# A hybrid decoder step: two head pairs of the prompt scan in one burst, the sample-diagonal products in a run of their own, and broadcasts from zero-padded rows

## The chip, the cores and the metric

The kernel runs on one NeuronCore of a Trainium2 chip. The metric is the device time of one execution in microseconds (us), lower is better.

## What is computed

Two layers of a hybrid trunk for 256 prompt tokens and 8 x 4 sample tokens, which share all weights. Each layer is a half-step SwiGLU feed-forward, a mixer of three branches (causal pooling, a Mamba-2 scan, attention into 256 memory tokens), and a second half-step feed-forward. The change touches the scan (`ssd_scan`), in chunks of 128 tokens, 16 heads of 64 channels, 4 groups of B and C with state 128:

```
xdt   = x * dt
decay = exp(where(causal, acum_t - acum_s, -inf))
y_diag = einsum('bcghts,bcsghp->bctghp', (C B^T) * decay, xdt)   # inside a chunk
states = einsum('bcsgn,bcsghp->bcghpn', B, xdt * to_end)         # the chunk's state
y = y_diag + y_off + D * x
```

The prompt has two chunks and no earlier state. The sample group has four new tokens for each of eight sequences, and an earlier state that is read for `y_off`.

## The kernel before

All activations lie as [128 channels, 288 tokens] (256 prompt, then 32 sample tokens). The 128x128 weight tiles are streamed past TensorE in slabs of eight. Each weight and each activation is split into two float32r parts, so one weight tile takes three products of 288 columns; the trace names them `ps`. Every slab is a tick (`Stream.tick`): ScalarE and VectorE split a later slab (`whi`, `wlo`), and `Stream.step` then advances each piece of side work that is under way by one stage (one `yield`), in the order in which the pieces were started. A piece may be started with a delay in ticks. The order on each engine is the order in which the program issues it (`manual_schedule`).

The scan's side work starts with the pooling columns (`kind == "u"`, `c == 0`), L1154 to L1158: `xss_work` after 3 ticks, the eight `sample_state` pieces from 8 on, `heads4(g)` after 4, 8, 12 and 16 ticks, `sample_y` after 28 and `group_norm` after 30. The ticks of the pooling columns (`pool_mix`) and of the `z` and gate columns run at the same time. `heads4(g)` takes the four heads of one group in two pairs, stage by stage:

1. four transposes of x (`ps_x`) and `rows(0)`
2. `xd = x * dt` and `xw` on VectorE and GpSimd, `clamp(0)`, `rows(1)`
3. `clamp(1)` on VectorE, the exponentials of both pairs on ScalarE (`E`)
4. the mask and C B^T multiplied into both `E` on VectorE
5. `outputs(0)` on TensorE
6. `finish(0)`, `outputs(1)`
7. `finish(1)`

Stage 5 of one group falls into the tick of stage 1 of the next. `rows(pi)` broadcasts two rows of `nst` (48 partitions: the high part of the cumulative sums in rows 0 to 15, the low part in 32 to 47) to all partitions, by two float32r products with a selecting column of `sel2` as weights. `outputs(pi)` writes one PSUM bank `ps_y`: two sample-diagonal products (`Ms`, 32 rows x 64 columns of the array, 32 tokens moving), six products with `E` (128 x 64, 128 tokens moving) that alternate between the halves j = 0 and 1 of the output partitions, and two products of full size for the state (`Bt`). A product of float32 operands shows as two passes in the trace, one of float32r as one. `finish(pi)` adds `D * x` on VectorE, copies the state out on ScalarE and issues its DMA on the queue of SP, which also issues the weight loads.

PSUM has seven banks under tag `b` for all of this and one under tag `a`. `dt_work` fills `nst`; GpSimd clears it there first, in each layer.

Of the kernel before, what the change touches and what calls it, by code (L numbers as in the profile page):

```python
# [44 lines left out]
def group_order(tiles, cuts):  # L45
    """Weight tiles (tile, k) of a group of products: all tiles up to each cut of k in turn."""
    for a, b in zip((0,) + cuts[:-1], cuts):
        for t in tiles:
            for k in range(a, b):
                yield t, k  # L50
# [56 lines left out]
class Stream:  # L107
    """Runs the packed weight tiles past TensorE, each split into two float32r parts.

    Every SLAB tiles make a tick: the split of a later slab is issued, then one stage  # L110
    of every piece of side work that is under way."""

# [8 lines left out]
    def parts(self, n):  # L121
        """The first slab comes in two halves, so that the products can begin."""
        k = 2 if n == 0 else 1
        return [slice(j * SLAB * P // k, (j + 1) * SLAB * P // k) for j in range(k)]
# [64 lines left out]
def trunk_kernel(ctx, tc, wpack, xT, memT, vecs, consts, wdt, wpool, hpool, hconv, h0T, kT, vC,  # L189
# [31 lines left out]
    def blocks(name):  # L221
        """Two tiles of zeros for block_fill()."""
        us = [unit(f"{name}{j}") for j in range(2)]
        for u in us:
            G.memset(u, 0.0)
        return us

    def block_fill(us, srcs, copy):
        """Block b of 32 columns, of each of the four slices, gets the slice's samples with all but sample b zero."""
        for u, src in zip(us, srcs):  # L230
            copy(u.rearrange("p a (b s) -> p a b s", b=DB)[:, :, :, 0:DL], src.rearrange("p a (b t) -> p a b t", b=DB))
# [55 lines left out]
    def chunk(units, c):  # L287
        return units[c // 2][:, c % 2, :]

    def products(tiles, cuts, xs):  # L290
        """One PSUM bank per tile: W[:, cols].T @ x."""
        ps = [bank("ps") for _ in tiles]
        for j, k in group_order(range(len(tiles)), cuts):
            mm3(ps[j][:, :T], W.take(), chunk(xs[0], k), chunk(xs[1], k), k == 0, k == cuts[-1] - 1)
        return ps
# [9 lines left out]
    def rstd_cols(accs, starts, width, name):  # L305
        """1 / sqrt(mean + eps) of the column sums of accs, tokens on partitions: [128, len(accs) * len(starts)]."""
        n = len(accs) * len(starts)
        ps = bank("ps_" + name)
        for a, acc in enumerate(accs):
            for j, s in enumerate(starts):  # L310
                k = a * len(starts) + j
                mm(ps[:, k:k + 1], acc[:, s:s + P], ones[:, 0:1])
        v = sp.tile([P, 12], F32, tag="rs_v", name="rs_v", bufs=2)[:, :n]
        ts(v, ps[:, :n], 1.0 / width, ALU.mult, EPS, ALU.add)
        r = sp.tile([P, 12], F32, tag="rs_r", name="rs_r", bufs=2)[:, :n]
        act(r, v, AF.Sqrt)
        V.reciprocal(out=r, in_=r)
        stt(v, v, -0.5, r, ALU.mult, ALU.mult)
        tt(v, v, r, ALU.mult)
        stt(r, v, 1.5, r, ALU.add, ALU.mult)  # L320
        return r

    def rstd_rows(r, t, sums, width):
        """r = 1 / sqrt(sums / width + eps), elementwise; stages."""
        yield
        ts(t, sums, 1.0 / width, ALU.mult, EPS, ALU.add)
        act(r, t, AF.Sqrt)
        yield
        V.reciprocal(out=r, in_=r)
        stt(t, t, -0.5, r, ALU.mult, ALU.mult)  # L330
        tt(t, t, r, ALU.mult)
        stt(r, t, 1.5, r, ALU.add, ALU.mult)
# [3 lines left out]
    def spread(r):  # L336
        """out[p, t] = r of token t, for every partition p; r holds tokens 0.., 128.., 160.. by column."""
        ps = bank("ps_spread")
        mm(ps[:, 0:P], r[:, 0:1].to_broadcast([P, P]), ident)
        mm(ps[:, P:TP], r[:, 1:2].to_broadcast([P, P]), ident)  # L340
        mm(ps[:, TP:T], r[:, 2:3].to_broadcast([P, P]), ident[:, P - TS:P])
        return ps

    class Norm:
        """Collects sum(x^2) chunk by chunk and splits x * gain for the products."""

# [22 lines left out]
    class Final:  # L369
        """The last norm: x * gain in place, then its scale and the output."""  # L370

# [38 lines left out]

# [1 line left out]
    mem = [unit(f"mem{j}") for j in range(KC // 2)]  # L412
# [16 lines left out]
    rv = cp.tile([P, 2], F32, name="rv")  # L429
    sel2 = cp.tile([48, H], F32R, name="sel2")  # L430
    sel4 = cp.tile([P, 4], F32R, name="sel4")
# [14 lines left out]
    def mem_norm():  # L446
# [13 lines left out]
        act(sel4, ident.rearrange("p (a b) -> p a b", a=4)[:, :, 0], AF.Copy)  # L460
        act(sel2, con[:48, K_SEL:K_SEL + H], AF.Copy)

# [62 lines left out]

# [1 line left out]
    def ffn(i, which, cur, nxt):  # L527
# [34 lines left out]

# [1 line left out]
    def mixer(i, cur, nxt):  # L564
# [42 lines left out]

        nst = sp.tile([48, TP], F32R, tag="nst", name="nst")
        nac = sp.tile([H, T], F32, tag="nac", name="nac")
# [20 lines left out]
        def dt_work(ps_dt):  # L630
# [4 lines left out]
            G.memset(v[:, 2, :], 0.0)  # L635
            G.memset(nst.bitcast(F32), 0.0)
            yield
# [11 lines left out]
            yield  # L649
            # log1p(e) = 2 atanh(e / (2 + e))  # L650
            ts(s, e, 2.0, ALU.add)
# [11 lines left out]
            yield  # L663
            # cumulative sums, heads on partitions and tokens on partitions; sums to the end of the group
            ph = bank("ps_nac")
# [93 lines left out]
        def xss_work():  # L759
# [16 lines left out]
            for q in range(2):  # L776
                act(xst[q][0:TS], xw[q], AF.Copy)
                act(xst[q][2 * TS:], xw[q], AF.Copy)
                tt(xst[q][TS:2 * TS], xw[q], xst[q][0:TS].bitcast(F32), ALU.subtract)

        def sample_state(b):
            hb = k4.tile([P, D], F32, tag="k4", name="hb")
# [31 lines left out]
        def heads4(g):  # L814
            """Four heads of the prompt's scan: two pairs of heads, one group of B and C."""
            hs = slice(4 * g, 4 * g + 4)

            def rows(pi):
                prow = bank("ps_row")
                for j in range(2):  # L820
                    h = 4 * g + 2 * pi + j
                    mm(prow[:, j * TP:(j + 1) * TP], sel2[:, h:h + 1].to_broadcast([48, P]), nst)
                return prow
# [16 lines left out]

            def outputs(pi, E):
                py = bank("ps_y")
                xb = 128 * pi

                def half(k, c, src, first, last):
                    for j in range(2):
                        x0 = k * TP + xb + 64 * j
                        mm(py[64 * j:64 * j + 64, c:c + P], xd[:, x0:x0 + 64], E[:, j, src:src + P], first, last)

                for j in range(2):  # L850
                    h = 4 * g + 2 * pi + j
                    mm(py[64 * j:64 * j + 64, TP:T], xss[h // 8][:, (h % 8) * 64:(h % 8 + 1) * 64], Ms[:, h, :])
                half(0, 0, 0, True, True)
                half(0, P, P, True, False)
                half(1, P, TP, False, True)
                mm(py[:, 320:448], xw[:, xb:xb + P], Bt[:, 0, g * P:(g + 1) * P], True, False)
                mm(py[:, 320:448], xw[:, TP + xb:TP + xb + P], Bt[:, 1, g * P:(g + 1) * P], False, True)
                return py

            def finish(pi, py):  # L860
                p = 2 * g + pi
                xp = chunk(xsu, p)
                st = tmp("st", P)
                stt(xp, xp, col(i, V_DS, p), py[:, :T], ALU.mult, ALU.add)
                act(st, py[:, 320:448], AF.Copy)
                nc.sync.dma_start(out=o_ssm_p[i, p], in_=st)
# [23 lines left out]
            yield  # L890
            y0 = outputs(0, E0)
            yield
            finish(0, y0)
            y1 = outputs(1, E1)
            yield
            finish(1, y1)

# [88 lines left out]
        def softmax(ps, n):  # L986
            """Rows of ps [128, n, 256] (scores) to weights; stages."""
            sc = P ** -0.5
# [152 lines left out]
        for kind, cs, tiles, cuts in mixer_groups():  # L1141
            c = cs[0]
            # side work that this group's products need, or that can begin here
            if kind == "q":
# [7 lines left out]
            if kind == "u" and c == 0:  # L1152
                W.pool_share = 0
                items["xss"] = W.start(xss_work(), 3)  # L1154
                items["ss"] = [W.start(sample_state(b), 8 + 2 * b) for b in range(DB)]
                items["pairs"] = [W.start(heads4(g), 4 + 4 * g) for g in range(4)]
                items["yo"] = W.start(sample_y(), 28)
                items["gn"] = W.start(group_norm(), 30)  # L1158
# [183 lines left out]
```

## Time and profile before

| | |
|---|---|
| median of three runs | 1600.78 us (1600.12 to 1602.69) |
| span of the profiled execution, first to last instruction | 1597.1 us |
| median less span | 3.7 us |
| busy: PE, PEld, DVE | 98%, 94%, 67% |
| busy: ACT, POOL | 50%, 19% |
| mean granted TensorE clock | 0.992 |

The profiled execution's device time is taken as its span and the same 3.7 us around it. PE is TensorE's products, PEld its weight loads, DVE VectorE, ACT ScalarE, POOL GpSimd. The ends of products are modelled and overlap the next product, so the distance from start to start tells what a product costs, not its duration.

### The profile page before, as it was taken

What the parts mean: (1) busy time and instruction counts of PE and PEld (TensorE: products, weight loads), DVE (VectorE), ACT (ScalarE), POOL (GpSimd) and SP (SyncE); (2) the same over time, 40 slices, a digit from 0 to 9 for tenths busy, and PEclk for the clock granted to TensorE, in tenths of its full rate; (3) what the DMA queues carried; (4) which work ended last, traced back from release to release, by engine and by line L of the source; (5) the groups of instructions that cost most, each with busy time, mean ns of one, the idle gap of its engine ahead of it and who ended that gap; (6) DMA issues with size and microseconds to landing.
All of it is one profiled execution on the core that took longest, in us unless ns stands there. A gap on an engine that the chain in (4) does not pass through costs nothing.

```text
span 1597.1 us, 29305 instructions
## 1 busy us (share of the span) xinstructions
PE 1558.0 (98%) x11792; PEld 1502.7 (94%) x11792; DVE 1066.3 (67%) x1598; ACT 804.0 (50%) x1231; POOL 302.9 (19%) x368
## 2 busy tenths in 40 slices
PE   7999999988999999999999999999999999999997
PEld 6899999887889999999999999988888999999997
DVE  6765645788777867656456665588778786766643
ACT  7444434465565546444445444456557454644442
POOL 3000001368233102000000000046823320200001
PEclk9999999999999999999999999999999999999999
DMA  6744444546465454444444444554655545444452
GB/s 244 230 167 166 164 165 171 196 147 233 168 212 193 147 173 167 162 165 166 165 166 160 171 161 169 178 185 151 238 170 188 203 159 169 158 168 167 159 171 70
DMA packets 81287, 278.00 MB, mean 174 GB/s; under 512 B 9088, under 2 KB 14336, under 8 KB 81152
## 3 DMA queue, kind: packets, MB, share of 16 engines
q1 hardware_dynamic: 81152, 276.14, 50.2%
q8 instruction: 92, 1.51, 0.4%
q14 instruction: 43, 0.35, 0.1%
HBM read 262.39 MB, written 13.71 MB: 173 GB/s over the span
## 4 chain that ended last, share of the span: by engine, by line
PE 87%; DVE 8%; ACT 2%; DMA 1%; POOL 1%; issue 1%; SPq 0%; DVEq 0%; ACTq 0%; POOLq 0%
PE ps L249 61%; PE pd L249 18%; DVE cacc L246 4%; PE ps_y L249 2%; PE ps_v L249 1%; PE ps_k L249 1%; ACT L252 1%; DMA raw<-wpack 1%; PE ps_up L249 1%; DVE wlo L148 1%; DVE cbuf L237 1%; ACT cacc L252 1%; PE ps_yo L249 1%; ACT whi L139 1%; PE ps_sp L249 0%
## 5 line engine op out<-in xcount | busy, mean ns | idle before, releaser
L148 DVE TENSOR_TENSOR wlo<-raw,whi 128x1024 fp32r<-128x1024 f32 (+1 forms) x409 | 517.8, 1267 | 266.8 <-ACT hidh L252 99.9
L139 ACT ACTIVATE whi<-raw 128x1024 fp32r<-128x1024 f32 (+1 forms) x441 | 463.7, 1054 | 329.3 <-PE ps L249 153.2
L249 PE MATMUL ps<-n1h,whi 128*128 128x288 f32 x896 | 274.4, 306 | 5.4 <-DVE Bst L237 5.4
L249 PE MATMUL ps<-n1h,wlo 128*128 128x288 f32 x896 | 266.9, 298 | 4.8 <-POOL wlo L148 4.8
L249 PE MATMUL ps<-n1l,whi 128*128 128x288 f32 x896 | 266.3, 297 | 0.0
L249 PE MATMUL ps<-n2h,whi 128*128 128x288 f32 x704 | 208.8, 297 | 0.0
L249 PE MATMUL ps<-n0h,whi 128*128 128x288 f32 x704 | 208.6, 296 | 0.0
L249 PE MATMUL pd<-hidh,whi 128*128 128x288 f32 x704 | 208.4, 296 | 0.0
L249 PE MATMUL ps<-n0l,whi 128*128 128x288 f32 x704 | 207.7, 295 | 0.0
L249 PE MATMUL pd<-hidl,whi 128*128 128x288 f32 x704 | 207.7, 295 | 0.0
L249 PE MATMUL ps<-n2l,whi 128*128 128x288 f32 x704 | 207.7, 295 | 0.0
L249 PE MATMUL ps<-n2h,wlo 128*128 128x288 f32 x704 | 207.0, 294 | 0.0
L249 PE MATMUL ps<-n0h,wlo 128*128 128x288 f32 x704 | 207.0, 294 | 0.0
L249 PE MATMUL pd<-hidh,wlo 128*128 128x288 f32 x704 | 207.0, 294 | 0.0
L237 POOL TENSOR_TENSOR acc<-acc,sqr 128x288 f32<-128x288 f32 x42 | 44.7, 1064 | 786.9 <-ACT sqr L252 785.9
L249 PEld LDWEIGHTS ps<-n1h,whi 128*128 128x128 f32 x896 | 170.3, 190 | 16.1 <-DVE Bst L237 5.8
L249 PEld LDWEIGHTS ps<-n1h,wlo 128*128 128x128 f32 x896 | 170.4, 190 | 7.3 <-POOL wlo L148 6.9
L249 PEld LDWEIGHTS ps<-n1l,whi 128*128 128x128 f32 x896 | 170.5, 190 | 0.7
L249 PEld LDWEIGHTS ps<-n0h,wlo 128*128 128x128 f32 x704 | 132.6, 188 | 0.0
L249 PEld LDWEIGHTS pd<-hidh,wlo 128*128 128x128 f32 x704 | 132.6, 188 | 0.0
L249 PEld LDWEIGHTS ps<-n2h,wlo 128*128 128x128 f32 x704 | 132.6, 188 | 0.0
L249 PEld LDWEIGHTS ps<-n2l,whi 128*128 128x128 f32 x704 | 132.1, 188 | 0.1
(297 smaller groups left out, 2877.5 us busy)
## 6 DMA issues: line engine op xcount, KB each, us to landing
raw<-wpack SPq DMA_DIRECT2D x439, 512.0 KB, 3.3
kb<-kT SPq DMA_DIRECT2D x16, 512.0 KB, 5.1
vb<-vC SPq DMA_DIRECT2D x16, 512.0 KB, 4.6
hb<-h0T SPq DMA_DIRECT2D x16, 512.0 KB, 5.8
o_ssm_s<-hb SPq DMA_DIRECT2D x16, 512.0 KB, 5.0
x<-xT SPq DMA_DIRECT2D x4, 288.0 KB, 4.1
o_y<-x SPq DMA_DIRECT2D x8, 144.0 KB, 1.8
mem<-memT SPq DMA_DIRECT2D x4, 256.0 KB, 4.6
```

The source lines that it names most:

```text
L139: nc.scalar.activation(out=hi[:, a], in_=self.loaded[self.n_hi][:, a], func=AF.Copy)
L148: eng.tensor_tensor(out=lo[:, a], in0=raw[:, a], in1=self.his[n][:, a].bitcast(F32), op=ALU.subtract)
L237: (eng or V).tensor_tensor(out=out, in0=a, in1=b, op=op)
L246: V.scalar_tensor_tensor(out=out, in0=a, scalar=s, in1=b, op0=op0, op1=op1)
L249: PE.matmul(out, lhsT=lhsT, rhs=rhs, start=start, stop=stop)
L252: A.activation(out=out, in_=a, func=func, **kw)
```

## The change

The two `outputs` of a group become one call, in the stage in which `outputs(0)` stood: 12 products with `E` for both pairs, then the four `Bt` products, into two banks. Both `finish` follow in the next stage, and the seventh stage goes. The 16 sample-diagonal products of a layer leave `outputs` for a new piece, `sample_diag`, which runs them one after the other into one bank and adds `D * x` of the sample tokens with eight small VectorE instructions; `finish` handles the prompt's 256 tokens only. `nst` and `sel2` grow from 48 to 128 partitions, the added rows are zero, and `nst` is cleared once, at the start of the program. The lines that the diff changes in comments and texts alone are left out.

```diff
-    sel2 = cp.tile([48, H], F32R, name="sel2")
+    sel2 = cp.tile([P, H], F32R, name="sel2")
+    nst = cp.tile([P, TP], F32R, name="nst")
+    G.memset(nst.bitcast(F32), 0.0)
...
-        act(sel2, con[:48, K_SEL:K_SEL + H], AF.Copy)
+        act(sel2, con[:, K_SEL:K_SEL + H], AF.Copy)
...
-        nst = sp.tile([48, TP], F32R, tag="nst", name="nst")
...
-            G.memset(nst.bitcast(F32), 0.0)
...
+        def sample_diag():
+            pd = bank("ps_yd")
+            for h in range(H):
+                p, j = divmod(h, 2)
+                mm(pd[64 * j:64 * j + 64, TS * p:TS * p + TS], xss[h // 8][:, (h % 8) * 64:(h % 8 + 1) * 64], Ms[:, h, :])
+            yield
+            for g in range(4):
+                xs = xsu[g][:, :, TP:T]
+                d = vec[:, i * V_N + V_DS + 2 * g:i * V_N + V_DS + 2 * g + 2]
+                tt(xs, xs, d.unsqueeze(2).to_broadcast([P, 2, TS]), ALU.mult)
+                tt(xs, xs, pd[:, 2 * TS * g:2 * TS * g + 2 * TS].rearrange("p (a t) -> p a t", a=2), ALU.add)
...
-                    mm(prow[:, j * TP:(j + 1) * TP], sel2[:, h:h + 1].to_broadcast([48, P]), nst)
+                    mm(prow[:, j * TP:(j + 1) * TP], sel2[:, h:h + 1].to_broadcast([P, P]), nst)
...
-            def outputs(pi, E):
...
+            def outputs(Es):
+                ys = [bank("ps_y") for _ in Es]
+                for pi, E in enumerate(Es):
+                    for k, c, src, first, last in ((0, 0, 0, True, True), (0, P, P, True, False), (1, P, TP, False, True)):
+                        for j in range(2):
+                            x0 = k * TP + 128 * pi + 64 * j
+                            mm(ys[pi][64 * j:64 * j + 64, c:c + P], xd[:, x0:x0 + 64], E[:, j, src:src + P], first, last)
+                for pi in range(2):
+                    for k in range(2):
+                        x0 = k * TP + 128 * pi
+                        mm(ys[pi][:, 320:448], xw[:, x0:x0 + P], Bt[:, k, g * P:(g + 1) * P], k == 0, k == 1)
+                return ys
...
-                xp = chunk(xsu, p)
+                xp = chunk(xsu, p)[:, :TP]
...
-                stt(xp, xp, col(i, V_DS, p), py[:, :T], ALU.mult, ALU.add)
+                stt(xp, xp, col(i, V_DS, p), py[:, :TP], ALU.mult, ALU.add)
...
-            y0 = outputs(0, E0)
-            yield
-            finish(0, y0)
-            y1 = outputs(1, E1)
-            yield
-            finish(1, y1)
+            ys = outputs((E0, E1))
+            yield
+            finish(0, ys[0])
+            finish(1, ys[1])
...
                 items["pairs"] = [W.start(heads4(g), 4 + 4 * g) for g in range(4)]
+                items["pairs"].append(W.start(sample_diag(), 7))
```

## Rows read from the trace of the kernel before

**Rows 1.** The page: busy us, share of the span and instructions of TensorE.
```profile
PE 1558.0 (98%) x11792; PEld 1502.7 (94%) x11792; DVE 1066.3 (67%) x1598; ACT 804.0 (50%) x1231; POOL 302.9 (19%) x368
```

**Rows 2.** TensorE's waits over the span: releaser, us in total, times, longest.
```profile
PE ps_pool L249 <- DVE pd L237: 5.4, 2, 2.7
```

**Rows 3.** Busy us of each engine in two stretches of layer 0.
```profile
382.00:396.00 14.00, 11.29 (x111) 9.53 (x110) 8.07 (x18) 7.33 (x12) 13.61 (x24) 0.97 0.63 253
400.00:500.00 100.00, 100.00 (x812) 88.93 (x812) 74.61 (x115) 57.17 (x112) 28.98 (x18) 1.00 0.56 190
```

**Rows 4.** Timeline of TensorE, one tick with `outputs(0)`, transposes and `rows(0)`: start, us.
```profile
406.07 0.29 PE L249 MATMUL ps<-n1h,wlo 128*128 128x288 f32 x1
406.29 0.30 PE L249 MATMUL ps_y<-Ms,xss 32*64 32x32 f32 x4
406.53 0.88 PE L249 MATMUL ps_y<-E,xd 128*64 128x128 f32 x12
407.33 0.71 PE L249 MATMUL ps_y<-Bt,xw 128*128 128x128 f32 x4
407.88 0.60 PE L872 MATMUL ps_x<-con,xs 128*128 128x128 f32 x4
408.41 0.49 PE L249 MATMUL ps_row<-nst,sel 48*128 48x256 f32 x2
...
409.21 0.29 PE L249 MATMUL ps<-n1h,wlo 128*128 128x288 f32 x1
409.34 0.29 PE L249 MATMUL ps<-n1h,whi 128*128 128x288 f32 x1
```

**Rows 5.** Timeline of TensorE at single instants: passes then under way, first start.
```profile
406.37 0.22 PE L249 MATMUL ps_y<-Ms,xss 32*64 32x32 f32 x2
...
407.01 0.39 PE L249 MATMUL ps_y<-E,xd 128*64 128x128 f32 x4
...
407.12 0.28 PE L249 MATMUL ps_y<-E,xd 128*64 128x128 f32 x2
...
407.66 0.39 PE L249 MATMUL ps_y<-Bt,xw 128*128 128x128 f32 x2
```

**Rows 6.** TensorE's groups by shape: count, busy us, mean ns.
```profile
L249 PE MATMUL ps_y<-E,xd 128*64 128x128 f32 x192 | 14.0, 281 | 0.0
...
L249 PE MATMUL ps_row<-nst,sel 48*128 48x256 f32 x32 | 7.9, 327 | 0.0
```

**Rows 7.** Timeline of TensorE: the last products of `sample_state`, 96 rows, and what follows.
```profile
419.61 0.40 PE L249 MATMUL ps_up<-xst,bm 96*128 96x256 f32 x2
419.85 0.30 PE L249 MATMUL ps<-n1h,whi 128*128 128x288 f32 x1
```

**Rows 8.** Timeline of TensorE, layer 0: the wait for the pooling branch, and after it.
```profile
395.84 1.30 PE L249 MATMUL ps_pool<-pd,wp 128*128 128x288 f32 x2 [2.71 <-DVE pd L237]
...
397.41 0.44 PE L249 MATMUL ps<-n1h,wlo 128*128 128x288 f32 x1
...
398.61 0.31 PE L249 MATMUL ps<-n1l,whi 128*128 128x288 f32 x1
```

**Rows 9.** Timeline of POOL ahead of that wait.
```profile
388.53 2.04 POOL L237 TENSOR_TENSOR xsw<-xss,wt 32x512 f32<-32x512 f32 x2
```

**Rows 10.** Timeline of DVE: ahead of that wait, two ticks later, and a small addition.
```profile
390.26 0.85 DVE L237 TENSOR_TENSOR xst<-xsw,xst 32x512 fp32r<-32x512 f32 x1 [5.37 <-ACT xst L252]
...
412.33 0.46 DVE L237 TENSOR_TENSOR z<-ps,R_n 128x288 f32<-128x288 f32 x1 [2.10 <-PE ps L249]
...
505.08 0.22 DVE L237 TENSOR_TENSOR xs<-xs,yoff 128x64 f32<-128x64 f32 x1
```

**Rows 11.** Timeline of TensorE: the second group's `outputs(0)` begins.
```profile
428.87 0.30 PE L249 MATMUL ps_y<-Ms,xss 32*64 32x32 f32 x4
```

**Rows 12.** Timeline of DVE in the tick of the second group's outputs.
```profile
430.74 1.28 DVE L237 TENSOR_TENSOR hb<-hb,ps_up 128x512 f32<-128x512 f32 x2
```

**Rows 13.** Timeline of ACT there: the copy of the first pair's state.
```profile
432.48 0.28 ACT L252 ACTIVATE st<-ps_y 128x128 f32<-128x128 f32 x1 [4.64 <-DVE xs L246]
```

More of the change, by code (lines that the diff above doesn't have):

```diff
@@ L839, in decay @@
                         act(e, e, AF.Exp, scale=-1.0, bias=nact[:, t_, h:h + 1])
-            def outputs(pi, E):
[L842 to L858, printed above, removed]
+            def outputs(Es):
[10 more added lines that the diff above has]
+                return ys
             def finish(pi, py):
                 p = 2 * g + pi
-                xp = chunk(xsu, p)
+                xp = chunk(xsu, p)[:, :TP]
                 st = tmp("st", P)
-                stt(xp, xp, col(i, V_DS, p), py[:, :T], ALU.mult, ALU.add)
+                stt(xp, xp, col(i, V_DS, p), py[:, :TP], ALU.mult, ALU.add)
                 act(st, py[:, 320:448], AF.Copy)
```

## The prediction

> **What bounds the kernel now.** I read the page first: TensorE is busy for 98% of the span [rows 1], so a change pays only where it shortens TensorE's own stream, or a wait in it. Next the waits: TensorE's largest in the stretch that the change touches is 2.7 us, twice, once in each layer, where a product of the pooling branch waits for VectorE [rows 2]. The busy times by stretch say what stands around it. From 382 to 396 us, ahead of that wait, TensorE is busy for 11.29 of 14 us and GpSimd for 13.61: GpSimd sets the pace there. From 400 to 500 us TensorE is busy without a gap, VectorE for 74.61 of 100 [rows 3]. So the scan has two parts: up to the wait TensorE has time to spare, behind it each microsecond of its stream is a microsecond of the kernel. Last the timeline of TensorE in one tick of the second part, for the price of each piece [rows 4], and at single instants for the pitch inside a run [rows 5]. I take prices from start to start.
>
> **The burst, first what a call costs now.** Large products follow each other at 0.13 us (409.21 to 409.34). From the last one (406.07) to the first sample-diagonal pass are 0.22 us, so 0.09 is lost at the entry. The four diagonal passes take 0.24 (406.29 to 406.53), the twelve passes with E 0.80 (to 407.33), the four Bt passes 0.55 (to 407.88). Sum 1.68 us a call [rows 4]. 192 E passes [rows 6] at 12 a call are 16 calls.
>
> Inside a run the E passes go in pairs, one for each half of the output partitions, at 0.11 us a pair (407.01 to 407.12), and a Bt pass takes 0.11 (two from 407.66 to 407.88) [rows 4, 5]. Six pairs at 0.11 are 0.66 of the 0.80, four Bt 0.44 of the 0.55: 0.14 and 0.11 are lost where the shape of the products changes. The merged call therefore costs 0.09 (entry) + 0.80 + 6 x 0.11 (E) + 0.55 + 4 x 0.11 (Bt) = 2.54 us, in place of 2 x 1.68 = 3.36. It saves 0.82 for each of 8 groups (4 in each layer): **-6.6 us**. Where the entry goes straight to E, no row shows it; bounds are no loss beyond the 0.09 and another 0.11 as at Bt, 0.9 us over eight; I take none more, since E's 0.14 already holds a slow first pair.
>
> **The diagonal run.** 32 passes a layer stand by themselves. The second pair of four starts 0.08 after the first (406.29, 406.37) [rows 4, 5], so 16 pairs take 1.28, the entry 0.09, the end of the last pair 0.08 more (406.37 to 406.53 is 0.16), and the first full-size pass behind it loses 0.11 as Bt's does: 1.56 us a layer, **+3.1 us**. Bounds: at most what a call pays for two heads now, 8 x 0.24 + 0.20 = 2.1 a layer, 4.2 in all; at least the E pair's pace scaled to 32 of 128 columns, 0.03 a pair, 0.48 + 0.28 = 0.76 a layer, 1.5 in all. I take the pitch that is there, for it is the same shape. The Trainium skill ("TensorE: Matmul & The Clock Gate", Back-to-back issue gap) gives about 60 cycles to any product of 1 to 64 columns, 25 ns at full clock. By that the 32 passes would take, as an estimate from that page, 0.80 us a layer in place of 1.28, and the sum would be 1.0 us lower; the row has 40 ns a pass and is what I use.
>
> **The padded rows.** One `rows` call: from the first transpose (407.88) to 409.34 are 1.46 us; four transposes at 0.11 and three large products at 0.13 leave 0.63 for two passes of 256 columns, what is lost before and after them included [rows 4]. The nearest row for a padded one is `ps_up`, also 256 columns of float32r, with 96 rows: 0.12 a pass, and the large product behind it starts without a loss [rows 7]. So a padded call costs 0.24 and saves 0.39. 32 passes [rows 6] are 16 calls, 6.2 us. But `heads4(0)` makes both of its calls ahead of the wait. There VectorE's `xst` sat idle for 5.37 us [rows 10] behind the products on GpSimd that end at 390.57 [rows 9], and pd stands behind `xst` on VectorE; the wait ends at 395.84 however early TensorE comes [rows 8]. Its two calls in each layer buy nothing: 12 x 0.39 = **-4.7 us**. Bounds: 0 if 128 rows cost as much as 48 do, -6.2 if nothing is swallowed.
>
> **What costs nothing, and its cover.** The eight small VectorE instructions of `sample_diag` are at most 0.22 each [rows 10], 1.8 us a layer, one tick after the products. In the next tick VectorE idles for 2.10 us before it takes TensorE's result [rows 10]; uncovered they would cost 2 x 1.8 less what the shorter `finish` gives back. No product but the last norm's reads what they write. The weight split queued behind them is for a slab two ticks ahead. The second `finish` comes one stage earlier: one addition, one copy, one DMA, at the same point of VectorE's, ScalarE's and SP's order as the first; the next weight load on SP stands behind both copies, as it stood behind one, and is issued five slabs ahead. GpSimd loses a clear of 48 rows in each layer and gains one of 128 at the start, where it has no work before the first loads land. The longest a piece is late is the tick of stage 5, by 2.54 - 1.68 - 0.39 = 0.5 us, and the following tick is shorter by 1.68 + 0.39; all pieces keep their ticks.
>
> **The sum.** -6.6 + 3.1 - 4.7 = -8.1 us with the terms unrounded. Against the profiled span of 1597.1 that is 1589.0; with the 3.7 us around it, against the median of 1600.78, **1592.7 us**.
>
> **The rivals.**
> *Padding buys nothing.* What a `rows` call loses could come from the change between float32 and float32r or from the broadcast weights, not from 48 rows. Against it: `ps_up` follows float32 work, is float32r, and has no loss behind it [rows 7]. Then -3.4, 1597.3.
> *The banks run out.* This is the one that could end slower. A burst now holds two banks where it held one, in a tick that also takes `ps_x`, `ps_row`, two for `ps_up`, one or two of the attention, and the product's own: eight or nine of seven, some still unread. TensorE would stand at `ps_x` or `ps_row` until VectorE has added the `ps_up` banks, which it does from 430.74 to 432.02 [rows 12], or until ScalarE has copied the first state at 432.76 [rows 13]. The tick's burst, begun at 428.87 [rows 11], would end at 431.4, transposes and row call at 432.1, so the wait is 0 to 1.3 us. There are six such ticks, three in each layer: at 1.3 each +7.8, 1600.5, no change. It decides beyond 1.35 (8.1 / 6) and is measurably slower from 1.9. For it: the count; against it: VectorE's readers do not depend on the blocked products, and before, TensorE waited for no bank in that tick though it needed seven.
> *TensorE is not the bound.* VectorE or GpSimd would set the ticks from 400 us on and swallow all: 1600.8. VectorE has a quarter of its time free there and waits for TensorE [rows 3, 10].
> *The clock.* Behind the wait large products run at 0.24 us in place of 0.13 (five from 397.41 to 398.61) [rows 8], the lower of the two levels, 1.2 GHz. TensorE will come 0.8 us sooner and wait 3.5 us in place of 2.7. If that doubles the slow stretch, whose loss here is about 1.4 us (2.8 us at half speed, 395.84 to 398.61), it costs 1.4 in each layer: 1595.5.
>
> **How the numbers follow.** Forecast 0.65 (its own range 1589 to 1595); padding in vain 0.08; banks 0.12, of which 0.04 slower; not the bound 0.07; clock 0.08. A difference under 0.2%, 3.2 us, can't be told from none here. Faster: 0.65 + 0.08 + 0.05 (padding, just beyond the bound) + 0.04 (banks, waits under 0.8 us) = 0.82. Slower: 0.04. The rest, 0.14, is no change. The favourable bounds together are -8.1 - 1.5 (nothing swallowed) - 1.6 (diagonal) = -11.2, 1589.6; the low end takes 1589.0 with the measurement's spread. The high end, 1598.5, holds the first rival and the clock, and leaves out TensorE not being the bound and the worse half of the banks.
>
> **What would show it.** Right: one entry to 24 E passes and 8 Bt passes, 2.5 us long together; 32 diagonal passes in about 1.3 us; `ps_row` with 128 rows, two at 0.12 us and the large product behind at 0.13; the wait for pd longer by about 0.8 us. Wrong: a new wait of TensorE for VectorE or ScalarE ahead of `ps_x`, `ps_row` or `ps` in the ticks of the bursts; large products at 0.24 us over more than some 3 us a layer; VectorE without idle time from 400 to 500 us.

## The result, and the profile after

The changed kernel takes 1591.28 us (median of four runs, 1590.19 to 1593.67), the kernel before 1600.72 beside it (1600.12 to 1602.69): a ratio of 0.9939 [0.9925, 0.9953], 9.4 us faster. The forecast was 1592.7. The profiled execution has a span of 1590.3 us and took 1592.05, so 1.75 us lie around this span, not 3.7.

On the page, the busy times: TensorE still fills 98% of the span, with as many instructions as before, in 6.5 us less [rows 1].

```profile
PE 1551.5 (98%) x11792; PEld 1504.2 (95%) x11792; DVE 1066.2 (67%) x1614; ACT 803.8 (51%) x1231; POOL 302.6 (19%) x367
```

The waits of TensorE: the one for `pd` (total, times, longest) is the only one in the stretch that the change touches. In each layer it is now 3.3 us where it was 2.7 [rows 2].

```profile
PE ps_pool L249 <- DVE pd L237: 6.5, 2, 3.3
```

The busy times by stretch (us, then busy us and count for PE, PEld, DVE, ACT, POOL, then the granted clock as a share, DMA share and GB/s): ahead of the wait GpSimd is still busy for 13.61 of 14 us, behind it TensorE still has no gap [rows 3]. The middle row is the stretch at the lower clock level behind the wait.

```profile
382.00:396.00 14.00, 11.50 (x117) 10.12 (x115) 8.11 (x16) 6.40 (x9) 13.61 (x22) 1.00 0.71 278
396.70:400.10 3.40, 3.34 (x12) 3.08 (x13) 3.40 (x7) 1.77 (x7) 2.88 (x2) 0.50 0.06 20
400.00:500.00 100.00, 100.00 (x844) 92.07 (x844) 77.57 (x131) 59.50 (x117) 29.00 (x18) 1.00 0.58 196
```

TensorE's timeline, from the wait to the second group's row call, for comparison with [rows 4, 7, 8]:

```profile
396.76 1.30 PE L249 MATMUL ps_pool<-pd,wp 128*128 128x288 f32 x2 [3.26 <-DVE pd L237]
...
403.77 1.12 PE L249 MATMUL ps_yd<-Ms,xss 32*64 32x32 f32 x32
404.82 0.75 PE L249 MATMUL ps_pool<-pd,wp 128*128 128x288 f32 x2
...
408.47 0.29 PE L249 MATMUL ps<-n1h,wlo 128*128 128x288 f32 x1
408.69 1.53 PE L249 MATMUL ps_y<-E,xd 128*64 128x128 f32 x24
410.15 1.16 PE L249 MATMUL ps_y<-Bt,xw 128*128 128x128 f32 x8
411.15 0.60 PE L880 MATMUL ps_x<-con,xs 128*128 128x128 f32 x4
411.50 0.48 PE L249 MATMUL ps_row<-nst,sel 128*128 128x256 f32 x2
411.82 0.29 PE L249 MATMUL ps<-n1h,whi 128*128 128x288 f32 x1
411.96 0.29 PE L249 MATMUL ps<-n1l,whi 128*128 128x288 f32 x1
```

The chain of work that ended last gives the same pieces end to end (start, us, what):

```profile
403.84 1.05 PE ps_yd L249 x32
...
408.76 2.55 PE ps_y L249 x32
411.31 0.44 PE ps_x L880 x4
411.75 0.24 PE ps_row L249 x2
```

Each piece of the forecast can be read here. The burst has one entry (408.47 plus 0.13 to 408.69, 0.09 lost), 24 passes with E, 8 with Bt, together 2.55 us. The row call is 0.24 us and the large product behind it comes without a loss (from `ps_x` to the second product behind the call, 411.15 to 411.96, are 0.81 us: four transposes at 0.11, one product at 0.13, and 0.24). The diagonal run is 32 passes in 1.05 us.

Where the time came from is seen from three marks in each layer, all of them starts of TensorE's products: the first `ps_x`, the pooling product that ends the wait for `pd`, and the first `ps_yot` behind the last group. In layer 0 they stand at 382.72, 395.84 and 499.97 us before, and at 383.68, 396.76 and 496.83 after. The first part is as long as before, 13.1 us in both layers. The second fell from 104.13 to 100.07 us, in layer 1 from 104.35 to 100.05: 8.4 us in all, and all of it behind the wait. The spans differ by only 6.8, because the changed kernel's profile lost time where the change touches nothing: the first products of the program, up to the feed-forward's `pd`, took 0.9 us longer, and the last norm's `ps_spread` 0.6 longer (1.49 us where it was 0.85). The marks are used below for each experiment.

### The profile page after: what moved, and what is told of

Its sections match the earlier page's. It is cut to its first block, busy times and chain, and to the rows that moved or that the text cites. A ratio compares the mean times of both kernels' runs of the same rounds, so it can differ in the third digit from the quotient of the medians.

```text
span 1590.3 us, 29327 instructions
## 1 busy us (share of the span) xinstructions
PE 1551.5 (98%) x11792; PEld 1504.2 (95%) x11792; DVE 1066.2 (67%) x1614; ACT 803.8 (51%) x1231; POOL 302.6 (19%) x367
## 4 chain that ended last, share of the span: by engine, by line
PE 84%; DVE 9%; ACT 3%; POOL 2%; issue 1%; DMA 0%; SPq 0%; DVEq 0%; ACTq 0%; POOLq 0%
PE ps L249 59%; PE pd L249 18%; DVE cacc L246 4%; PE ps_y L249 1%; PE ps_v L249 1%; PE ps_k L249 1%; POOL pw L237 1%; DVE wlo L148 1%; ACT L252 1%; DVE cbuf L237 1%; PE ps_up L249 1%; ACT cacc L252 1%; PE ps_yo L249 1%; DMA raw<-wpack 0%; PE ps_sp L249 0%
## 5 line engine op out<-in xcount | busy, mean ns | idle before, releaser
L249 PEld LDWEIGHTS ps<-n0l,whi 128*128 128x128 f32 x704 | 132.2, 188 | 0.1
```

The source lines that it names most:

```text
L249: PE.matmul(out, lhsT=lhsT, rhs=rhs, start=start, stop=stop)
```

## The experiments

The kernel before was measured beside each group of runs, at 1600.4 to 1600.9 us; each ratio is against it.

### The padded rows by themselves

The kernel before, with `sel2` and `nst` on 128 rows, cleared once:

```diff
-    sel2 = cp.tile([48, H], F32R, name="sel2")
+    sel2 = cp.tile([P, H], F32R, name="sel2")
+    nst = cp.tile([P, TP], F32R, name="nst")
...
-                    mm(prow[:, j * TP:(j + 1) * TP], sel2[:, h:h + 1].to_broadcast([48, P]), nst)
+                    mm(prow[:, j * TP:(j + 1) * TP], sel2[:, h:h + 1].to_broadcast([P, P]), nst)
```

> The kernel before with nothing changed but the 128-partition rows of nst and sel2. My theory: a rows call costs 0.63 us with 48 rows and 0.24 with 128, because the 48-row shape is another shape than the products around it; the four calls ahead of the pooling wait buy nothing. From the end of that wait to the first ps_yot 104.1 to 104.4 us become about 101.9 in each layer (6 x 0.39 = 2.3 less), the stretch from the first ps_x to the end of the wait stays at 13.1, and the time falls by 4.7 us, to 1596.0. Rival, the burst brought all of the gain and the padding nothing: 1600.7. Rival, nothing is swallowed by the wait: 6.2 us less, 1594.5.

Measured 1596.17 us (1595.43 to 1596.68), 0.9968 [0.9955, 0.998]: 4.5 us, against 4.7 forecast. The first mark to the wait's end is 13.09 us in both layers, as long as before, while the wait grew:

```profile
PE ps_pool L249 <- DVE pd L237: 3.3, 1, 3.3
```

So the two calls ahead of it buy nothing. They save 0.39 and 0.19 us of TensorE's stream (from `ps_x` at 382.72 to the first large product behind the call and `ps_pool`, 1.39 us before and 1.00 here; from `ps_row` at 388.18 to the first large product behind `ps_pool`, 0.80 before and 0.61 here), and the wait takes both. From the wait's end to `ps_yot` layer 1 has 102.03 us where it had 104.35, the 2.3 less that six calls should give. Layer 0 has 103.31: the clock stayed at its lower level there for nearly twice as long (see the last section).

### How many rows count as full

The changed kernel with 64 rows, and with 96, in `sel2`, `nst` and the broadcast:

```diff
-    sel2 = cp.tile([P, H], F32R, name="sel2")
-    nst = cp.tile([P, TP], F32R, name="nst")
+    sel2 = cp.tile([64, H], F32R, name="sel2")
+    nst = cp.tile([64, TP], F32R, name="nst")
...
```

> The changed kernel with nst and sel2 of 64 partitions in place of 128. The rows were cheap with 128 and dear with 48, and ps_up with 96 showed no loss. My theory: what is dear is a shape that leaves half of the array's rows out; 64 rows are then as dear as 48: two passes start 0.2 us apart, the large product behind them loses 0.1 and more, a call costs 0.63 us, and the stretch from the pooling wait to ps_yot is 2.3 us longer in each layer than in the changed kernel. Rival: 48 is dear because it is no multiple of 32; then 64 rows cost 0.24 as 128 do.

> The changed kernel with nst and sel2 of 96 partitions. My theory: 96 rows count as the full array, a call costs 0.24 us as with 128, and the stretch from the pooling wait to ps_yot is that of the changed kernel, but for the clock. Rival: any number of rows below 128 is another shape: 0.63 us a call, 2.3 us more in each layer.

One run each: 1595.61 us with 64 rows, 1591.55 with 96. TensorE's timeline of the 64-row kernel around one call:

```profile
411.55 0.60 PE L880 MATMUL ps_x<-con,xs 128*128 128x128 f32 x4
412.08 0.50 PE L249 MATMUL ps_row<-nst,sel 64*128 64x256 f32 x2
412.51 0.40 PE L249 MATMUL ps<-n1h,whi 128*128 128x288 f32 x1
412.74 0.30 PE L249 MATMUL ps<-n1l,whi 128*128 128x288 f32 x1
```

and of the 96-row kernel:

```profile
410.63 0.60 PE L880 MATMUL ps_x<-con,xs 128*128 128x128 f32 x4
410.98 0.48 PE L249 MATMUL ps_row<-nst,sel 96*128 96x256 f32 x2
411.30 0.30 PE L249 MATMUL ps<-n1h,whi 128*128 128x288 f32 x1
411.44 0.29 PE L249 MATMUL ps<-n1l,whi 128*128 128x288 f32 x1
```

From `ps_x` to the second product behind the call are 1.19 us and 0.81 us. Less the four transposes (0.44) and one product (0.13) a call costs 0.62 and 0.24: 64 rows are as dear as 48 were, 96 as cheap as 128. Nearly all of the loss lies on both sides of the call, not in its passes, which start 0.22 and 0.20 us apart. The longer stretch shows it too: from the wait's end to `ps_yot` the 96-row kernel has 100.13 and 100.06 us, as the changed kernel has, and the 64-row kernel 102.47 in layer 0, 2.4 more; in its layer 1, 100.89, the clock did not fall. The Trainium skill ("TensorEngine Tiling (Array Packing)", Tiling Modes and Key Properties) lists modes of 128, 64 and 32 rows and says that changing the mode drains the engine. The traces agree so far that a change of shape costs time here, 0.38 us for going in and coming back, and that 96 rows cost what 128 do; that the lost time is a drain can't be read from them.

### The order inside the burst

The changed kernel with the pairs one behind the other inside the call (E, Bt, E, Bt):

```diff
                 for pi, E in enumerate(Es):
                     for k, c, src, first, last in ((0, 0, 0, True, True), (0, P, P, True, False), (1, P, TP, False, True)):
                         ...
-                for pi in range(2):
                     for k in range(2):
```

> The changed kernel with one edit: both pairs still in one stage, but in the order E of pair 0, Bt of pair 0, E of pair 1, Bt of pair 1. The count of products is the same, the shape changes two times more in each group. My theory, the shape changes are the price: 0.09 at the entry, 0.14 in E, 0.11 at Bt once more for each of 8 groups, 0.34 x 8 = 2.7 us more than the changed kernel, 1594.0; a group's y products take 2.9 us in place of 2.55. Rival, what counts is that the calls share a tick: no difference, 1591.3 and 2.55 us.

Measured 1595.8 us (1593.91 to 1596.61), 0.9963 [0.9951, 0.9976]. Its timeline of one burst, and then its chain:

```profile
408.12 0.88 PE L249 MATMUL ps_y<-E,xd 128*64 128x128 f32 x12
408.93 0.71 PE L249 MATMUL ps_y<-Bt,xw 128*128 128x128 f32 x4
409.57 0.88 PE L249 MATMUL ps_y<-E,xd 128*64 128x128 f32 x12
410.37 0.71 PE L249 MATMUL ps_y<-Bt,xw 128*128 128x128 f32 x4
410.92 0.60 PE L879 MATMUL ps_x<-con,xs 128*128 128x128 f32 x4
```

```profile
408.19 2.90 PE ps_y L249 x32
```

2.90 us in place of 2.55, with the same passes: one more round of shape changes costs 0.35 us, 2.8 over eight groups. From the wait's end to `ps_yot` it has 101.28 us in both layers where the changed kernel has 100.07 and 100.05, 2.4 us in all; the medians differ by 4.5, more than the trace, but the runs range over 2.7 and 3.5 us. So the price of the shapes is shown, and its size is better read from the chain than from the medians.

### The diagonal products back in the burst

The changed kernel without `sample_diag`; the four products stand at the head of each burst, and `finish` takes all 288 tokens again:

```diff
+                for pi in range(2):
+                    for j in range(2):
+                        h = 4 * g + 2 * pi + j
+                        mm(ys[pi][64 * j:64 * j + 64, TP:T], xss[h // 8][:, (h % 8) * 64:(h % 8 + 1) * 64], Ms[:, h, :])
                 for pi, E in enumerate(Es):
...
-                items["pairs"].append(W.start(sample_diag(), 7))
```

> The changed kernel with sample_diag taken out and the four diagonal products of a group put back, as a run at the head of the group's burst. My theory: a pass of the diagonal run costs 0.033 us and entering and leaving the shape some 0.2 us in all; eight passes at the head of a burst are 0.26, leaving the shape 0.1, the entry is paid by the burst already. So 0.36 x 4 = 1.4 us a layer in place of 1.24 for the run of its own: within 0.5 us of the changed kernel, 1591.6, and the run of its own is worth next to nothing once the pairs are merged. Rival, the separate run is a main source of the gain: the diagonal costs what it cost before, 0.24 for two heads and 0.2 more, over 2.6 us a layer, and the time rises by 2.8 us or more, to 1594.1.

Measured 1591.33 us (1590.87 to 1593.74), 0.9943 [0.9931, 0.9956]: no different from the whole change. Its timeline of one burst:

```profile
407.36 0.29 PE L249 MATMUL ps<-n1h,wlo 128*128 128x288 f32 x1
407.59 0.42 PE L249 MATMUL ps_y<-Ms,xss 32*64 32x32 f32 x8
407.94 1.53 PE L249 MATMUL ps_y<-E,xd 128*64 128x128 f32 x24
```

Eight diagonal passes take 0.35 us there, four times in a layer 1.40; in a run of their own they cost 1.24 with what is lost on both sides. That is 0.3 us over both layers, too little for the medians to show. From the wait's end to `ps_yot` layer 0 has 100.20 us where the changed kernel has 100.07, which agrees; layer 1 has 98.68, because the clock did not fall there at all, behind a wait of the same 3.27 us. A burst with its diagonal takes 2.55 + 0.35 = 2.90 us, against 3.36 for the two calls before: eight times 0.46, 3.7 us, come from merging the pairs, and 0.3 from moving the diagonal out of the burst.

### The banks: the diagonal one tick earlier

The changed kernel, with `sample_diag` started one tick sooner:

```diff
-                items["pairs"].append(W.start(sample_diag(), 7))
+                items["pairs"].append(W.start(sample_diag(), 6))
```

> The changed kernel with sample_diag started one tick earlier, so that its products fall into the wait for the pooling branch. My theory: TensorE stands idle for 3.3 us there whatever it has done before, so the 1.24 us a layer that the run costs behind the wait become free: the wait shrinks to about 2.1 us, the stretch behind it is 1.2 us shorter in each layer, the time falls by 2.5 us, to 1588.8. Rival: the eight small VectorE instructions, now one tick earlier, where VectorE is 90% busy, push back what the wait is for or the tick behind it by what is won: 1591.3.

Measured 1594.89 us (1593.23 to 1596.07), 0.9963 [0.9951, 0.9976]: by the medians 3.6 us slower than the changed kernel, not faster. The theory was that the diagonal run fills part of the wait for `pd`. TensorE's timeline of it:

```profile
392.93 1.12 PE L249 MATMUL ps_yd<-Ms,xss 32*64 32x32 f32 x32 [0.33 <-DVE xd L237]
395.84 1.33 PE L249 MATMUL ps_pool<-pd,wp 128*128 128x288 f32 x2 [1.79 <-DVE z L237]
398.57 0.61 PE L249 MATMUL ps<-n1h,whi 128*128 128x288 f32 x1 [1.40 <-DVE ypl L246]
```

and VectorE's, where `pd` and `z` end:

```profile
395.23 0.19 DVE L237 TENSOR_TENSOR pd<-pf,ub 128x7 f32<-128x7 f32 x1
395.34 0.45 DVE L237 TENSOR_TENSOR z<-ps,R_n 128x288 f32<-128x288 f32 x1
```

The run does fill part of the wait, but `pd` still ends only at 395.42: most of the 1.79 us would be there for `pd` alone. What is new is that the pooling product goes on behind VectorE's `z`, some 0.3 us later, and that the next product waits 1.40 us for `ypl`. Neither `z` nor `ypl` is an input of the product that waits; each reads a bank, `z` one of `ps` and `ypl` one of `ps_pool`, and `ps_yd` has taken a bank one tick earlier. This fits the rival on the banks; which bank each product took is not in the trace, so the cause is argued and not shown. In the change itself no such wait exists. With the new wait what the run won is lost again, and the slow stretch behind the waits is twice as long as in the changed kernel; from the first mark to `ps_yot` are 114.2 us where it has 113.2.

```profile
395.40:398.70 3.30, 1.46 (x3) 0.63 (x3) 3.30 (x6) 1.67 (x7) 2.98 (x3) 0.50 0.11 12
398.80:402.10 3.30, 3.30 (x15) 3.30 (x16) 3.27 (x8) 2.83 (x7) 0.00 (x0) 0.50 0.79 239
```

### The wait ahead: four tries to end it on GpSimd's side

GpSimd is busy for 13.61 of 14 us ahead of the wait, so its `xsw`, 2.04 us, was moved to VectorE (first edit), then moved with buffers of its own as well (second):

```diff
-                   wt[:TS, 2, 8 * q:8 * q + 8].unsqueeze(2).to_broadcast([TS, 8, 64]), ALU.mult, G)
+                   wt[:TS, 2, 8 * q:8 * q + 8].unsqueeze(2).to_broadcast([TS, 8, 64]), ALU.mult)
```

```diff
-            xw = [wide("xsw", TS) for q in range(2)]
+            xw = [ep.tile([P, 2, 3 * P], F32, tag="E", name="xsw").rearrange("p j t -> p (j t)")[:TS, :512] for q in range(2)]
```

> The changed kernel with one edit: the two products xsw of xss_work run on VectorE, not on GpSimd (2.04 us there). My theory: the wait of 3.3 us for the pooling branch stands behind xst, which waits for xsw on a GpSimd that is busy without a gap; with xsw on VectorE, idle for 5.4 us there, xst is done before the wait, the wait goes, the clock stays at its upper level behind it, and the two rows calls ahead of it now pay. 3.3 us of wait and about 1.4 us of half speed in each layer: 9.4 us less than the changed kernel, 1582, and ps_x to the pooling product about 9.8 us in place of 13.1. Rival, the pooling windows on GpSimd themselves bind (pw of the third group): the wait shrinks by less than 1 us and the clock still falls, 1590 to 1591.

> xsw_dve again, with one edit more: the two xsw take buffers of E, which are free then, not those that they shared with the pooling windows pw. In xsw_dve the second xsw waited 3.2 us for a pw on GpSimd, and everything behind it on VectorE came late; the first did not wait. My theory: without that shared buffer both run at once, xst is done at about 390 us, pd of the third window by 393, before TensorE asks for it; the wait and the half-speed stretch go: 3.3 and some 1.6 us in each layer, 9 to 10 us less than the changed kernel, 1582. Rival: GpSimd's pw bind, or VectorE itself, slowed by GpSimd next to it (pd took 0.85 us apiece beside GpSimd and 0.25 without), is late by as much: the wait stays over 2 us, 1589 to 1592.

Measured 1593.54 us (1593.16 to 1595.36), 0.9957 [0.9943, 0.9971], and 1591.23 (1590.42 to 1593.45), 0.9943 [0.9929, 0.9956]. Both theories fell: the wait stayed, at 3.1 and 2.9 us. VectorE's timeline, first edit:

```profile
387.69 0.68 DVE L237 TENSOR_TENSOR xsw<-xss,wt 32x512 f32<-32x512 f32 x1 [3.20 <-POOL pw L237]
```

and with both edits:

```profile
393.97 0.69 DVE L237 TENSOR_TENSOR xd<-ps_x,dtt 128x512 f32<-128x512 f32 x1 [2.40 <-POOL pw L237]
...
396.63 0.97 DVE L237 TENSOR_TENSOR pd<-pf,ub 128x7 f32<-128x7 f32 x1
```

VectorE, freed of the wait for `xsw`, stands behind GpSimd's pooling sums `pw` in another place. `xsw` and `xd` read nothing of `pw`; they share its ring of scratch tiles (`wide`), so a new tile waits until GpSimd has done with an old one. With buffers of its own `xsw` waits no longer, and `xd` does instead: the ring couples the two engines whichever of them does `xsw`.

Then the pooling sums of groups 2 and 3 went to VectorE, and those of group 2 alone (`g != 2`):

```diff
-                tt(nx[:, lo + step:UC], at[:, lo + step:UC], at[:, lo:UC - step], ALU.add, G)
+                tt(nx[:, lo + step:UC], at[:, lo + step:UC], at[:, lo:UC - step], ALU.add, G if g < 2 else V)
```

> The changed kernel with the window sums pw of the pooling groups 2 and 3 on VectorE, not on GpSimd; xsw stays on GpSimd in its old buffers. In both xsw kernels VectorE ended up waiting 2.4 to 3.2 us for a buffer that a pw on GpSimd held. My theory: the wait of TensorE is GpSimd's queue, by whichever way VectorE meets it; without the seven sums (5.8 us there beside VectorE) GpSimd reaches xsw 2.7 us sooner, VectorE does its seven in about 4 us that it idled, pd of group 2 is ready at 392, before TensorE asks at 393.4, and the wait and the half-speed stretch behind it go: 3.3 and 1.6 us in each layer, 1581.5. Rival: VectorE is late by its own queue now, the wait stays over 2 us: 1589 to 1592.

> As pw_dve, with group 2 alone on VectorE (three sums). My theory: xsw comes 2.7 us sooner on GpSimd, so the wait of 3.3 us shrinks to under 1 us; the clock may still fall; 1583 to 1587. Rival: the buffers of the pooling windows bind again: 1589 to 1592.

Measured 1594.19 us (1591.52 to 1594.74), 0.9955 [0.9942, 0.9969], and 1592.09 (1590.26 to 1593.24), 0.9946 [0.9934, 0.9959]. The waits are 3.6 and 3.0 to 3.1 us. With both groups on VectorE it is busy for 13.16 of the 13.5 us from 384.9 on, and `pd` comes at the end of them. None of the four shifts of work between these two engines ended the wait.

### The pooling product one tick later

The other end of the wait: one `yield` more ahead of `ps_pool`, so that VectorE and GpSimd have a tick longer. In the changed kernel, and in the kernel before:

```diff
                 tt(d[:, :w - 1], f[:, :w - 1], u[:, 15:14 + w], ALU.subtract)
             yield
+            yield
             pq = bank("ps_pool")
```

> The changed kernel with one yield more in pool_mix, so that the pooling product is issued one tick later; nothing else moves. Four edits did not make VectorE's pd earlier. My theory now: the wait of 3.3 us is not a shortage of work for TensorE, but that the product stands in TensorE's queue a tick before its operand can be there, with products that are ready behind it. Issued a tick later its operand is long there; the results are needed only some ten ticks on. The wait and the half-speed stretch behind it go: 3.3 + 1.6 us in each layer, 9.8 us less than the changed kernel, 1581.5. Rival: VectorE is late for all that follows too, and TensorE waits in that tick or the next for a split weight (wlo) or a bank instead: 1586 to 1591.

> The kernel before with the same one yield. It tells whether the wait swallowed the rows calls ahead of it. My theory: the wait of 2.7 us and about 1.5 us of half speed go in each layer, 8.4 us less than before, 1592.3; and the step from this kernel to pool_later is larger than from before to after, by the two rows calls of 0.39 us in each layer: some 10.3 us, where the clock's share taken out before to after was 8.7. Rival, nothing was swallowed: the two steps are equal, 8.7.

Measured 1587.46 us (1586.62 to 1589.12), 0.992 [0.9907, 0.9932], for the changed kernel, and 1594.82 (1593.86 to 1595.09), 0.9963 [0.9949, 0.9976], for the one before. The first is the fastest of all kernels here: no run of it is as slow as the fastest of the changed kernel (1590.19), though the two intervals against before overlap. But it falls in the range of its rival, not at the 1581.5 forecast. Its waits of TensorE from 380 to 500 us:

```profile
PE ps_x L880 <- DVE xs L237: 0.8, 1, 0.8
PE ps L249 <- ACT whi L139: 0.5, 1, 0.5
PE ps_pool L249 <- DVE z L237: 0.4, 1, 0.4
```

Its clock by stretch, where the wait and the slow stretch had been:

```profile
393.00:396.00 3.00, 2.47 (x28) 1.85 (x21) 2.97 (x5) 2.94 (x4) 2.76 (x4) 1.00 0.01 3
396.00:399.00 3.00, 3.00 (x34) 2.61 (x33) 2.96 (x5) 1.72 (x6) 3.00 (x5) 1.00 0.00 0
```

The wait for `pd` is gone, and so is the slow stretch behind it. From the first mark to `ps_yot` it has 110.65 us, the changed kernel 113.16: 2.5 us a layer. The wait and the slow stretch were worth 3.26 + 1.65 = 4.9 us; three new waits take 1.7 back, and 0.7 are not accounted for. In the longest new one `ps_x` waits for the last of the eight small instructions of `sample_diag`, which the prediction had held to be covered in that tick: VectorE runs them from 406.56 to 408.27 and TensorE goes on at 408.41. Whether `ps_x` wants the bank that they read or the tile that they write was not tried.

Between the two kernels with the `yield` the change is worth 4.0 us a layer (114.64 to 110.65), 7.4 by the medians. That is neither the 10.3 forecast nor its rival's 8.7. With no wait for `pd` to swallow them the row calls should all count: half of the 8.7 us that the change is worth without the clock (summed below), and 0.39 + 0.19 more, 4.9 a layer. But the changed one has 1.7 us of new waits, the other 0.9, which leaves 4.1. The 4.0 measured are near that, and 0.4 more than if two calls were still swallowed; but 0.5 to 0.8 us a layer are not accounted for in each of the two, so this pair supports the swallowing and does not settle it. The mark that the padded rows did not move does.

## Why the prediction was right

By its own steps:

**The burst.** 2.54 us were worked out and 2.55 measured; 8 x 0.81 = -6.5 us. The step that took E's 0.14 to hold a slow first pair was right: going straight to E loses 0.09 and no more. The order inside it confirmed the cause, shape changes: a second round of them costs 0.35.

**The diagonal run.** This is the one term of the sum that was mis-sized. 1.56 us a layer was forecast, from the pitch of 0.08 a pair between the first two pairs of a call. The run takes 1.05, 33 ns a pass, and with 0.09 at its head and 0.10 behind it 1.24: +2.5 us in place of +3.1. (From `ps_sp` to the large product behind the pooling product are 2.48 us, from 402.71 to 405.19, and 1.23 in the same tick of the kernel with the diagonal in the burst, from 402.87 to 404.10.) The 0.08 was the step from the first pair to the second, and that is the slow one: in the long run it is 0.08 as well (403.77 to 403.85), and the pairs behind it follow at 0.06. The Trainium skill's 25 ns for so few columns ("TensorE: Matmul & The Clock Gate", Back-to-back issue gap) lies below the 33 that the row has, the forecast's 40 above.

**The padded rows.** 0.24 a call, as forecast, and -4.7 us; by itself the edit gave 4.5. What `ps_up` showed for 96 rows [rows 7] holds for these as well. The two calls ahead of the wait bought nothing, as argued; the wait grew by 0.55, not 0.8, since the second of them, which stands between `ps_av` and `ps_pool`, saves only 0.19.

**What costs nothing.** This held: the eight small VectorE instructions run from 406.31 to 408.03, and VectorE still waits 0.35 us for TensorE's product ahead of `z` at 408.80.

**The sum.** -6.5 + 2.5 - 4.7 = -8.7, and the stretch between the marks is shorter by 8.4. The other 0.3 is the clock: half of the time that TensorE worked at the lower level behind the wait is lost, before 1.39 us (395.84 to 398.61) and 1.64 in layer 1, after 1.65 and 1.7. From the median of 1600.78 the 8.4 lead to 1592.4; 1591.28 was measured, and the other 1.1 us, which no stretch accounts for, is within the spread of the runs. So the number was met in part by luck: a diagonal run 0.6 us too dear in the sum stood against 0.3 of clock that it left out.

**Its footing.** The 3.7 us around the span was an error that cancelled out: 1.75 lie around it in the changed kernel and 1.7 to 1.8 in every experiment. So, as an estimate from these, about 1.9 of the 3.7 were an execution faster than the median, not time around it. Since sum and median were both carried with the same 3.7, the forecast did not suffer, but a span of 1589.0 was not to be expected and did not come.

**The rivals.** Padding that buys nothing is refuted by its own run. The banks did not run out; one edit of one tick brought waits that look like it. TensorE is the bound behind the wait. The clock did not double its slow stretch here; with the padding alone it nearly did in layer 0, see the last section.

## What to carry to other kernels

Count the changes of shape in a stream of products, not only the passes. Here one more round of them cost 0.35 us, so products of one shape belong together; and a call with 48 or 64 rows between full-size products was 0.38 to 0.39 dearer than one padded with zeros to 96 or 128. What is saved ahead of a wait is swallowed by it, so find the wait's other end first: here one more stage before the waiting product beat all four shifts of work between two engines that share a ring of scratch tiles. And when a piece moves to another tick, count the banks that it holds there.

## What the hardware showed that was not expected

**The slow stretch is not set by the wait alone.** Behind a wait of about 3 us the clock was at its lower level, 1.2 GHz, for 3.4 us, for nearly twice that, or not at all. In the kernel with `xsw` on VectorE in its own buffers the wait is 2.91 us in both layers. Its busy times behind them, layer 0 and layer 1:

```profile
398.00:401.00 3.00, 3.00 (x13) 2.82 (x13) 3.00 (x5) 1.12 (x5) 0.58 (x1) 0.54 0.13 20
...
1153.90:1157.00 3.10, 3.02 (x21) 2.94 (x22) 3.10 (x5) 1.21 (x5) 0.92 (x1) 1.00 0.03 11
```

From the wait's end to `ps_yot` these are 100.08 and 98.55 us, 1.5 us apart. In the other kernel with `xsw` on VectorE, with waits of 3.1 us, they are 101.32 and 98.55. The padding alone had 3.3 us of wait in both layers, and in layer 0 a slow stretch nearly twice as long as the changed kernel's behind the same wait; with the diagonal in the burst the same wait left layer 1 without one. So in these kernels the level after a wait near 3 us can't be forecast from its length, and differences of 1.5 us a layer between two profiles of such kernels should be read with the granted clock beside them.

**VectorE stands still behind GpSimd.** In that same kernel (`xsw` on VectorE in its own buffers) VectorE's operation on 7 columns, `pd<-pf,ub`, took 0.97 us from 396.63; the same instruction took 0.17 us with the pooling sums on VectorE, where GpSimd was idle when it began. Beside the slow one GpSimd ran `xw`, also an operation on two tensors, until 397.59:

```profile
396.55 1.04 POOL L237 TENSOR_TENSOR xw<-xd,wt 128x512 f32<-128x512 f32 x1
```

VectorE's next instruction came at 397.53. The Trainium skill ("SBUF — State Buffer", SBUF: two separate sides) says that these two engines share a pair of ports, and that, where VectorE's operation has two inputs in SBUF, the one which comes second is held for the other's whole instruction; the row agrees. By that the work moved from GpSimd to VectorE is not fully parallel to what stays there. It may be one more reason why none of the four tries paid; how much of each it cost was not measured.
